# The first 28 pairs of a hybrid layer with activations stationary, and two jobs of POOL on VectorE

## The chip, the cores and the metric

The kernel runs on one core of one Trainium2 chip. The metric is the device time of one execution in microseconds (us); three runs of the kernel before gave 2392.42, 2395.93 and 2392.65, median 2392.65.

The core has five engines that run beside each other and wait for one another through semaphores: TensorE (PE; its weight loads are PEld), VectorE (DVE), ScalarE (ACT), GpSimd (POOL) and SyncE (SP), which here issues the DMAs.

## The reference

One layer on 256 positions of width 2048, in float32: a feed-forward, a mixer (differential attention beside a gated delta rule) and a second feed-forward. Each is preceded by a shift and scale and followed by a gate, a residual and a layer norm; shift, scale and gate come from c through `w_ada`.

```python
def swiglu_ffn(h, w_in, w_out):
    g, u = jnp.split(h @ w_in, 2, axis=-1)
    return (jax.nn.silu(g) * u) @ w_out

ada = (silu(c) @ w_ada[l] + b_ada[l]).reshape(B, 3, 3, D)
shift, scale, gate = ada[:, :, 0, None], ada[:, :, 1, None], ada[:, :, 2, None]
y = swiglu_ffn(x * (1 + scale[:, 0]) + shift[:, 0], w_ffn_in[l, 0], w_ffn_out[l, 0])   # 2048 -> 2*5632 -> 2048
x = layer_norm(ALPHA * x + 0.5 * gate[:, 0] * y, ln_g[l, 0], ln_b[l, 0])
y = hybrid_mixer(x * (1 + scale[:, 1]) + shift[:, 1], ...)
x = layer_norm(ALPHA * x + gate[:, 1] * y, ln_g[l, 1], ln_b[l, 1])
y = swiglu_ffn(x * (1 + scale[:, 2]) + shift[:, 2], w_ffn_in[l, 1], w_ffn_out[l, 1])
x = layer_norm(ALPHA * x + 0.5 * gate[:, 2] * y, ln_g[l, 2], ln_b[l, 2])
```

## The kernel before

**Split products.** A float32 matrix is split into a high part (`hi`, rounded by ACT) and a low part (`lo` = raw - hi, by VectorE or POOL). A product takes three matmuls, hi·hi, hi·lo and lo·hi (`mm3`, lines 147 to 149), summed in a PSUM bank of 512 columns.

**Weights.** All weights come in one planned order as chunks of 128 x 1024 (512 KB). SP loads a chunk into one of six `raw` buffers, ACT writes `hi`, VectorE or POOL `lo` (`_split`), into one of four buffers each; PE reads them and frees the buffer. `k.pool_lo` says which engine makes the low part: 0 VectorE, 1 POOL for every chunk, 2 POOL for every second. Instructions go through a helper, so nearly all of VectorE, ACT and POOL show as line 88.

**Two forms of product.** With weights stationary, a matmul loads 128 x 128 of a chunk and streams h, 256 columns; a chunk is 24 matmuls (`_products`). With activations stationary, it loads 128 x 128 of h and streams 512 columns of weights; a chunk is 12 matmuls (`_xprod`, `_xstat`). The results of the first lie hidden by token, as the next product wants them; those of the second lie token by hidden and are turned by PE transposes (`hT`).

**The first stage.** h, the input of the first feed-forward, isn't there at the start: its 16 tiles come one by one (`_first_h`): four ada chunks (`sar`) each, four VectorE dots, `hf` on VectorE, `h_hi` on ACT, `h_lo` on POOL. Meanwhile the first 28 of the 44 pairs (a pair is 128 columns of g and of u) are computed in six visits (`VISITS`): each takes the tiles of h that are there, and adds its bank to an accumulator in SBUF (`acc`). `START_LO` gives the visits' `pool_lo`. A pair's last visit ends in `_ffn_hid`: add (VectorE), silu (ACT), multiply (VectorE), hi (ACT), lo (VectorE). The other 16 pairs of this feed-forward, and all of the last one, are made four at a time with activations stationary (`_ffn_block`, with `hT`).

**Beside the products.** `_Ada` makes the later shifts, scales and gates: per chunk `ar` two `acc<-ar,cs` steps on VectorE; a finished quarter of a gate is split (`acchi`, `acclo`) and summed over partitions by two matmuls of PE, `aps`. `_load_x` fetches the residual x for the mixer's and the last feed-forward's end and applies the norm's g and b, row by row (`rowg`, `rowb`): on POOL, 16 instructions each time. `_Next` makes the next layer's h at a layer's end; its stage 0 sets `pool_lo` to 1, so POOL makes the low parts during the last output product, and its `rest` sets it back.

**What sets the order.** The program keeps a model time `k.t`, which advances with PE's products; the rest are threads that yield how long they need, and after each `mm3` the threads that are due issue their next instructions. The order on each engine is fixed by this when the program is built.

Of the kernel before, what the change touches and what calls it, by code (L numbers as in the profile page):

```python
# [744 lines left out]
def _ffn_hid(k, ps, hid, j, acc=None, back=1):  # L745

    hid.job(j, k.read(_ffn_hid_run(k, ps, hid, j, acc, hid.all[-1:]), back))


def _ffn_hid_run(k, ps, hid, j, acc, before):  # L750
    u = k.uid()
    g, up = ps[:, 0, :], ps[:, 1, :]
    if acc is not None:
# [1 line left out]
        k.V.tensor_tensor(acc, acc, ps, ALU.add)
        g, up = acc[:, 0, :], acc[:, 1, :]
    yield 0.2
    while not all(th.done for th in before):
        yield 0.3
    sg = k.hp.tile([128, S], F32, tag="sg", name=f"sg{u}", bufs=2)  # L760
    k.A.activation(sg, g, AF.Silu)
    yield
    hf = k.hp.tile([128, S], F32, tag="hidf", name=f"hidf{u}", bufs=2)
    k.V.tensor_tensor(hf, sg, up, ALU.mult)
    yield
    both = k.hp.tile([128, 2, S], F32R, tag=f"hid{j}", name=f"hid{u}")
    hid[0][j], hid[1][j] = both[:, 0, :], both[:, 1, :]
    k.A.activation(hid[0][j], hf, AF.Copy)
    yield
    k.V.tensor_tensor(hid[1][j], hf, hid[0][j].bitcast(F32), ALU.subtract)  # L770


def _ffn_block(k, h, hid, b, before, pre):
# [36 lines left out]
    if pre is None:  # L810
        _xstat(k, KT // 2, h, gate)
    else:
        for t in range(2):
            k.read(gate(t, pre[t], 0, 512), 2 - t)
    _xstat(k, KT // 2, h, up)
# [675 lines left out]
def tile_hybrid_block(ctx: ExitStack, tc: tile.TileContext, names, aps):  # L1491
# [83 lines left out]
    def start(h, hid, side):  # L1575

        with ExitStack() as st:
# [5 lines left out]
            accs = [k.hp.tile([128, 2, S], F32, tag=f"hid{j}", name=f"acc{j}") for j in range(hid.ready)]  # L1583
            k.pool_lo = 1
            for (kt0, n, ja, jb), lo in zip(VISITS, START_LO):
                h.need(k, kt0)
# [1 line left out]
                npair, nchunk = max(1, 4 // n), max(1, n // 4)
                last = kt0 + n == KT
                for j0 in range(ja, jb, npair):  # L1590
                    pss = [k.bank([128, 2, S], "mms") for q in range(npair)]
                    for c in range(nchunk):
                        w = [x.rearrange("p (q r) -> p q r", q=npair) for x in k.weights()]
                        for q, ps in enumerate(pss):
                            _products(k, ps, [x[:, q, :] for x in w], kt0 + 4 * c, n // nchunk, [h, h], c == 0,
                                      c == nchunk - 1)
                    for q, ps in enumerate(pss):
                        j = j0 + q
                        if last:
                            _ffn_hid(k, ps, hid, j, accs[j], npair - q)  # L1600
                        else:
                            k.read(add(accs[j], ps, kt0 == 0), npair - q)
                    if last and first is not None:
                        k.wait(lambda: first.done)
                        first = None
                        _ada_keep(k)
                        st.close()
                        ada = side()
# [64 lines left out]
def _layout(inputs, np):  # L1673
# [40 lines left out]
    for kt0, n, ja, jb in VISITS:
        m, q = min(n, 4), max(1, 4 // n)
        w = wi[0][kt0 * 128:(kt0 + n) * 128, ja * 256:jb * 256].reshape(n // m, m, 128, (jb - ja) // q, q, 256)
        first.append(w.transpose(3, 0, 2, 4, 1, 5).reshape(-1, 128, 1024))
# [47 lines left out]
```

## Time and profile before

| | |
|---|---|
| median of three runs | 2392.65 us |
| the profiled execution | 2389.68 us, span 2387.9 |
| PE busy | 2305.5 us, 97% |
| PEld busy | 2071.9 us, 87% |
| VectorE busy | 1707.0 us, 71% |
| ACT busy | 1033.1 us, 43% |
| POOL busy | 329.1 us, 14% |
| DMA | 581.7 MB, mean 244 GB/s |
| chain that ended last | PE 86%, VectorE 7%, issue 2% |
| first and last matmul of the first stage | 15.6 and 360.7 us |

Busy time is no proof of a bound: a busy PE can be slow or fast, and an engine at 70% can be late at one place. So the pace of a product is read from how far apart its chunks stand, a stall from a window in which PE is less than fully busy, and its cause from what PE waited for there. "Clock" is the share of TensorE's full clock that was granted.

### The profile page before, as it was taken

The numbers are of one execution on the slowest core, as the hardware profiler recorded it, in microseconds if no ns is written. First come the engines' busy times: TensorE is split into PE (matmuls) and PEld (weight loads), VectorE is DVE, ScalarE is ACT, GpSimd is POOL, SyncE is SP. The second block draws the span as 40 slices with busy tenths as digits, with TensorE's granted clock in tenths as the row PEclk, the third lists the DMA queues.
The fourth block names the chain that finished last, engine by engine and source line by source line (L and its number), as shares of the span: only waits on it lengthen the run. The fifth ranks groups of instructions, "written<-read, shape, count | busy, mean of one in ns | idle before, by whom it ended". The sixth has DMA issues, their size and how long they took to land.

```text
span 2387.9 us, 36796 instructions
## 1 busy us (share of the span) xinstructions
PE 2305.5 (97%) x14217; PEld 2071.9 (87%) x14217; DVE 1707.0 (71%) x2508; ACT 1033.1 (43%) x1390; POOL 329.1 (14%) x218
## 2 busy tenths in 40 slices
PE   6999999999999899999999999999999999999997
PEld 6999997888888889988999999987878888888886
DVE  5667888787775688878887887786787555544556
ACT  4434444434444444454444434444444443444432
POOL 5884000000001310000000220013050000000001
PEclk8999999999999999999999999999999999999999
DMA  9998878899875566454546888876888556655553
GB/s 362 332 327 292 300 250 274 305 339 322 315 267 189 176 204 209 157 173 149 170 162 244 298 296 306 286 282 204 310 302 309 189 192 194 193 187 192 188 187 111
DMA packets 166359, 581.70 MB, mean 244 GB/s; under 512 B 19820, under 2 KB 22812, under 8 KB 165416
## 3 DMA queue, kind: packets, MB, share of 16 engines
q1 hardware_dynamic: 166184, 579.36, 70.7%
q8 instruction: 111, 1.82, 0.3%
q14 instruction: 64, 0.52, 0.1%
HBM read 572.98 MB, written 7.88 MB: 243 GB/s over the span
## 4 chain that ended last, share of the span: by engine, by line
PE 86%; DVE 7%; issue 2%; DMA 1%; POOL 1%; ACT 1%; SPq 0%; DVEq 0%; ACTq 0%; POOLq 0%
PE mx L148 17%; PE mx L147 17%; PE mx L149 17%; PE mm L147 6%; PE mm L148 6%; PE mm L149 6%; PE mms L148 4%; PE mms L149 4%; PE mms L147 4%; DVE lo L88 2%; DVE acc L88 1%; PE UY L153 1%; DVE x L88 1%; ACT hi L88 1%; PE hT L158 1%
## 5 line engine op out<-in xcount | busy, mean ns | idle before, releaser
L88 ACT ACTIVATE hi<-raw 128x1024 fp32r<-128x1024 f32 x769 | 811.6, 1059 | 968.7 <-PE mx L149 669.3
L88 DVE TENSOR_TENSOR lo<-raw,hi 128x1024 fp32r<-128x1024 f32 x690 | 855.7, 1246 | 495.7 <-ACT hi L88 485.4
L147 PE MATMUL mx<-hi,h_hi 128*128 128x512 f32 x992 | 389.7, 393 | 0.0
L149 PE MATMUL mx<-hi,h_lo 128*128 128x512 f32 x992 | 387.2, 390 | 0.0
L148 PE MATMUL mx<-lo,h_hi 128*128 128x512 f32 x992 | 387.0, 390 | 0.0
L147 PE MATMUL mm<-h_hi,hi 128*128 128x256 f32 x1216 | 354.4, 291 | 0.0
L149 PE MATMUL mm<-h_hi,lo 128*128 128x256 f32 x1216 | 346.5, 285 | 3.4 <-DVE lo L88 3.4
L148 PE MATMUL mm<-h_lo,hi 128*128 128x256 f32 x1216 | 346.4, 285 | 0.0
L88 POOL TENSOR_TENSOR lo<-raw,hi 128x1024 fp32r<-128x1024 f32 x79 | 190.2, 2415 | 788.0 <-ACT hi L88 788.0
L147 PE MATMUL mx<-hi,hid 128*128 128x512 f32 (+1 forms) x768 | 285.1, 371 | 1.4 <-ACT hi L88 1.4
L148 PE MATMUL mx<-lo,hid 128*128 128x512 f32 (+1 forms) x768 | 284.7, 371 | 0.8 <-DVE lo L88 0.8
L149 PE MATMUL mx<-hi,hid 128*128 128x512 f32 (+1 forms) x768 | 284.5, 370 | 0.0
L147 PE MATMUL mms<-h_hi,hi 128*128 128x256 f32 x896 | 256.2, 286 | 10.2 <-ACT hi L88 5.9
L148 PE MATMUL mms<-h_lo,hi 128*128 128x256 f32 x896 | 256.2, 286 | 3.7 <-POOL h_lo L88 3.7
L149 PE MATMUL mms<-h_hi,lo 128*128 128x256 f32 x896 | 255.9, 286 | 1.6 <-POOL lo L88 1.6
L149 PEld LDWEIGHTS mm<-h_hi,lo 128*128 128x128 f32 x1216 | 235.2, 193 | 3.9 <-DVE lo L88 3.9
L147 PEld LDWEIGHTS mm<-h_hi,hi 128*128 128x128 f32 x1216 | 235.7, 194 | 1.7 <-issue 1.6
L148 PEld LDWEIGHTS mm<-h_lo,hi 128*128 128x128 f32 x1216 | 235.7, 194 | 0.7 <-issue 0.6
L149 PEld LDWEIGHTS mx<-hi,h_lo 128*128 128x128 f32 x992 | 186.6, 188 | 39.2
L147 PEld LDWEIGHTS mx<-hi,h_hi 128*128 128x128 f32 x992 | 186.7, 188 | 38.2 <-issue 0.2
L148 PEld LDWEIGHTS mx<-lo,h_hi 128*128 128x128 f32 x992 | 186.7, 188 | 38.0 <-issue 0.2
L147 PEld LDWEIGHTS mms<-h_hi,hi 128*128 128x128 f32 x896 | 174.4, 195 | 10.9 <-ACT hi L88 6.1
(304 smaller groups left out, 3236.2 us busy)
## 6 DMA issues: line engine op xcount, KB each, us to landing
raw<-in_w_ffn_in_dram SPq DMA_DIRECT2D x240, 512.0 KB, 4.7
raw<-in_w_ffn_out_dram SPq DMA_DIRECT2D x176, 512.0 KB, 4.1
raw<-in_w_first_dram SPq DMA_DIRECT2D x112, 512.0 KB, 5.0
ar<-in_w_gate_dram SPq DMA_DIRECT2D x96, 512.0 KB, 5.1
ar<-in_w_ada_dram SPq DMA_DIRECT2D x96, 512.0 KB, 5.1
sar<-in_w_ada_dram SPq DMA_DIRECT2D x64, 512.0 KB, 5.0
raw<-in_w_gab_dram SPq DMA_DIRECT2D x64, 512.0 KB, 4.5
raw<-in_w_kq_dram SPq DMA_DIRECT2D x32, 512.0 KB, 3.6
```

The source lines that it names most:

```text
L88: return f(*args, **kw)
L147: mm(ps, lhsT=lhs[0], rhs=rhs[0], start=start, stop=False, skip_group_check=True)
L148: mm(ps, lhsT=lhs[0], rhs=rhs[1], start=False, stop=False, skip_group_check=True)
L149: mm(ps, lhsT=lhs[1], rhs=rhs[0], start=False, stop=stop, skip_group_check=True)
L153: self.nc.tensor.matmul(ps, lhsT=lhsT, rhs=rhs, start=start, stop=stop, skip_group_check=True)
L158: self.nc.tensor.transpose(ps, src, self.ident if ident is None else ident)
```

## The change

**The first stage.** `VISITS` now counts blocks of four pairs (0 to 7) and the visits run with activations stationary: a new `_xbanks` makes two banks (one for each half of the tokens) from the chunks of a visit, for g and for u. The columns of all visits, the count of chunks and the adds into `acc` are as before; `w_first` is laid out to match. `_ffn_hid` goes: a block's last visit ends in `_ffn_block`, which adds to `acc` (`summed`), applies silu and multiply on 512 columns, and turns the result on PE (`hT`).

**The affine part.** In `_load_x` the sixteen products and sums with `rowg` and `rowb` go from POOL to VectorE, and each waits 2 us of model time for itself.

**A layer's end.** `pool_lo` is not set to 1 in `_Next.step`; the low parts there are VectorE's. The setting ahead of the first visit goes as well, so the first two low parts of the kernel are VectorE's.

```diff
-VISITS = ((0, 2, 0, 28), (2, 2, 0, 28), (4, 4, 0, 28), (8, 4, 0, 12), (8, 8, 12, 28), (12, 4, 0, 12))
+VISITS = ((0, 2, 0, 7), (2, 2, 0, 7), (4, 4, 0, 7), (8, 4, 0, 3), (8, 8, 3, 7), (12, 4, 0, 3))
...
+def _xbanks(k, kt0, n, act, name="mx"):
+
+    pss = [k.bank([128, 512], name) for _ in range(2)]
+    for c in range(n // 2):
+        w = k.weights()
+        for j in range(2):
+            for t in range(2):
+                _xprod(k, pss[t], w, act, kt0 + 2 * c + j, j, t, 0, 512, kt0 + n - 1, kt0)
+    return pss
...
         if stage == 0:
-            k.pool_lo = 1
             self.A = None
...
-        yield 8.0
+        yield 4.0
         for t in range(2):
-            k.P.tensor_tensor(x[t][:, sl], x[t][:, sl], g, ALU.mult)
-            k.P.tensor_tensor(x[t][:, sl], x[t][:, sl], b, ALU.add)
+            for v, op in ((g, ALU.mult), (b, ALU.add)):
+                yield 2.0
+                k.V.tensor_tensor(x[t][:, sl], x[t][:, sl], v, op)
...
-def _ffn_block(k, h, hid, b, before, pre):
+def _ffn_block(k, hid, b, before, banks, accs=None):
     sg = {}
-    def gate(t, ps, lo, hi):
+    def summed(i, t, ps):
+        if accs is None:
+            return ps
+        acc = accs[4 * b + 2 * i + t]
+        k.V.tensor_tensor(acc, acc, ps, ALU.add)
+        return acc
+
+    def gate(t, ps):
         yield 0.2
+        src = summed(0, t, ps)
         while not all(th.done for th in before):
             yield 0.3
         sg[t] = k.hp.tile([128, 512], F32, tag=f"sg{t}", name=f"sg{k.uid()}")
-        k.A.activation(sg[t], ps, AF.Silu)
+        k.A.activation(sg[t], src, AF.Silu)
-    def up(t, ps, lo, hi):
+    def up(t, ps):
         yield 0.2
-        k.V.tensor_tensor(sg[t], sg[t], ps, ALU.mult)
+        src = summed(1, t, ps)
+        while t not in sg:
+            yield 0.3
+        k.V.tensor_tensor(sg[t], sg[t], src, ALU.mult)
...
-            k.pool_lo = 1
-            for (kt0, n, ja, jb), lo in zip(VISITS, START_LO):
+            for (kt0, n, ba, bb), lo in zip(VISITS, START_LO):
                 h.need(k, kt0)
                 k.pool_lo = lo
...
+                for b in range(ba, bb):
+                    if kt0 + n < KT:
+                        for i in range(2):
+                            for t, ps in enumerate(_xbanks(k, kt0, n, h, "mms")):
+                                k.read(add(accs[4 * b + 2 * i + t], ps, kt0 == 0), 2 - t)
+                        continue
...
+                    _ffn_block(k, hid, b, hid.all[-1:], banks, accs)
```

What stands in PE's order near the end of the first stage, in the last visit, around the `aps` pair of a gate's quarter. `mms` is a bank of the stage. Before:

```order
L147 MATMUL mms_4066<-h_hi_91,hi_3950 128x256
L148 MATMUL mms_4066<-h_lo_92,hi_3950 128x256
L149 MATMUL mms_4066<-h_hi_91,lo_3951 128x256
L153 MATMUL aps_4108<-acchi_4095,ones 128x512
L153 MATMUL aps_4108<-acclo_4096,ones 128x512
L147 MATMUL mms_4115<-h_hi_91,hi_3988 128x256
L148 MATMUL mms_4115<-h_lo_92,hi_3988 128x256
L149 MATMUL mms_4115<-h_hi_91,lo_3989 128x256
```

After:

```order
L147 MATMUL mms_2816<-hi_2741,h_hi_91 128x512
L148 MATMUL mms_2816<-lo_2742,h_hi_91 128x512
L149 MATMUL mms_2816<-hi_2741,h_lo_92 128x512
L153 MATMUL aps_2859<-acchi_2834,ones 128x512
L153 MATMUL aps_2859<-acclo_2835,ones 128x512
L158 MATMUL hT_2863<-ident,sg_2811 128x128
L158 MATMUL hT_2863<-ident,sg_2813 128x128
L158 MATMUL hT_2863<-ident,sg_2811 128x128
L158 MATMUL hT_2863<-ident,sg_2813 128x128
L147 MATMUL mms_2868<-hi_2770,h_hi_91 128x512
```

The `aps` pair now follows the two g banks of the last visit's second block; behind it come the first transposes of the block ahead of it, whose `sg` VectorE writes.

The affine part in the mixer's last part. Before it is in POOL's order (`x_13896` and `x_13897` are the two halves of the residual):

```order
L88 TENSOR_TENSOR x_13896<-x_13896,rowg_14315 128x512
L88 TENSOR_TENSOR x_13896<-x_13896,rowb_14316 128x512
L88 TENSOR_TENSOR x_13897<-x_13897,rowg_14315 128x512
L88 TENSOR_TENSOR x_13897<-x_13897,rowb_14316 128x512
L88 TENSOR_TENSOR x_13896<-x_13896,rowg_14430 128x512
```

After, in VectorE's order, between low parts and the ada gate's steps:

```order
L88 TENSOR_TENSOR lo_13052<-raw_12842,hi_13051 128x1024
L88 SCALAR_TENSOR_TENSOR acc_12854<-ar_12882,cs,acc_12854 128x512 x2
L88 TENSOR_TENSOR x_12552<-x_12552,rowg_12971 128x512
L88 TENSOR_TENSOR lo_13087<-raw_12888,hi_13086 128x1024
L88 TENSOR_TENSOR x_12552<-x_12552,rowb_12972 128x512
L88 TENSOR_TENSOR x_12553<-x_12553,rowg_12971 128x512
L88 TENSOR_TENSOR lo_13122<-raw_12921,hi_13121 128x1024
L88 TENSOR_TENSOR x_12553<-x_12553,rowb_12972 128x512
L88 SCALAR_TENSOR_TENSOR acc_12854<-ar_13007,cs,acc_12854 128x512 x2
L88 TENSOR_TENSOR lo_13161<-raw_12951,hi_13160 128x1024
```

Eight of the sixteen stand ahead of the next `acclo` there, eight behind it.

The end of the first layer in VectorE's order: the last low parts, and the residual of the output product's first tail piece. Before:

```order
L88 SCALAR_TENSOR_TENSOR res_7560<-mx_7376,gate_2789 128x512
L88 TENSOR_TENSOR x_2816<-x_2816,res_7560 128x512
L88 BN_STATS st_93<-x_2816 128x6 x2
L88 SCALAR_TENSOR_TENSOR res_7751<-mx_7539,gate_2789 128x256
L88 TENSOR_TENSOR x_2815<-x_2815,res_7751 128x256
```

After:

```order
L88 TENSOR_TENSOR lo_6330<-raw_6155,hi_6329 128x1024
L88 TENSOR_TENSOR lo_6360<-raw_6173,hi_6359 128x1024
L88 TENSOR_TENSOR lo_6390<-raw_6203,hi_6389 128x1024
L88 SCALAR_TENSOR_TENSOR res_6407<-mx_6195,gate_1986 128x256
L88 TENSOR_TENSOR x_2013<-x_2013,res_6407 128x256
```

The low parts of the last output product, which POOL made, stand ahead of the tail's first `res`.

## Rows read from the trace of the kernel before

**Rows 1.** Timeline of POOL, first stage (start, us, engine, line, operation, shape, idle before).
```profile
140.85 7.15 POOL L88 TENSOR_TENSOR lo<-raw,hi 128x1024 fp32r<-128x1024 f32 x3 [0.21 <-ACT hi L88]
...
154.30 0.74 POOL L88 TENSOR_TENSOR h_lo<-hf,h_hi 128x256 fp32r<-128x256 f32 x1 [0.68 <-DMA raw<-in_w_first_dram]
155.25 7.15 POOL L88 TENSOR_TENSOR lo<-raw,hi 128x1024 fp32r<-128x1024 f32 x3 [0.21 <-ACT hi L88]
```

**Rows 2.** Timeline of ACT, first layer, output product with 512 columns.
```profile
755.65 1.06 ACT L88 ACTIVATE hi<-raw 128x1024 fp32r<-128x1024 f32 x1 [1.66 <-PE mx L149]
758.37 1.06 ACT L88 ACTIVATE hi<-raw 128x1024 fp32r<-128x1024 f32 x1 [1.66 <-PE mx L149]
```

**Rows 3.** Windows: stretch, length, PE, PEld, DVE, ACT, POOL busy, clock, DMA share, GB/s.
```profile
100.00:150.00 50.00, 50.00 (x418) 49.97 (x418) 34.40 (x52) 18.98 (x20) 43.88 (x21) 1.00 0.92 335
...
300.00:350.00 50.00, 45.59 (x356) 44.79 (x355) 42.97 (x63) 21.80 (x34) 0.00 (x0) 0.93 0.75 251
350.00:400.00 50.00, 45.99 (x242) 38.58 (x241) 42.06 (x59) 23.11 (x34) 0.00 (x0) 1.00 0.81 267
...
1350.00:1400.00 50.00, 46.69 (x361) 45.89 (x361) 46.73 (x40) 18.96 (x22) 26.80 (x15) 0.93 0.79 267
1400.00:1450.00 50.00, 48.74 (x402) 48.18 (x401) 42.02 (x51) 20.38 (x25) 0.00 (x0) 1.00 0.90 317
```

**Rows 4.** Windows of 5 us, columns as above.
```profile
45.00:50.00 5.00, 5.00 (x44) 5.00 (x43) 2.35 (x5) 3.31 (x5) 4.39 (x2) 1.00 1.03 409
...
335.00:340.00 5.00, 2.70 (x9) 2.10 (x10) 3.97 (x7) 2.13 (x5) 0.00 (x0) 0.63 0.75 229
...
1755.00:1760.00 5.00, 3.32 (x14) 2.20 (x12) 4.96 (x5) 2.11 (x3) 3.63 (x3) 1.00 0.98 349
1760.00:1765.00 5.00, 4.48 (x20) 3.71 (x21) 4.96 (x4) 1.66 (x2) 3.77 (x2) 1.00 0.88 350
```

**Rows 5.** Waits of PE, 290 to 400: total us, times, longest.
```profile
PE aps L153 <- ACT acchi L88: 4.4, 2, 3.5
PE aps L153 <- DVE acclo L88: 1.9, 2, 1.0
```

**Rows 6.** Timeline of VectorE (DVE), end of the first stage.
```profile
310.24 1.22 DVE L88 TENSOR_TENSOR lo<-raw,hi 128x1024 fp32r<-128x1024 f32 x1
...
313.49 1.23 DVE L88 TENSOR_TENSOR lo<-raw,hi 128x1024 fp32r<-128x1024 f32 x1 [1.10 <-ACT hi L88]
...
316.41 1.22 DVE L88 TENSOR_TENSOR lo<-raw,hi 128x1024 fp32r<-128x1024 f32 x1
...
337.35 0.69 DVE L88 TENSOR_TENSOR acclo<-acc,acchi 128x512 fp32r<-128x512 f32 x1
```

**Rows 7.** Chain of waits, last feed-forward: start, us, what.
```profile
1732.39 0.44 PE hT L158 x4
```

**Rows 8.** Timeline of POOL, affine part in the mixer: first and last of sixteen.
```profile
1347.01 2.27 POOL L88 TENSOR_TENSOR x<-x,rowg 128x512 f32<-128x512 f32 x1 [65.41 <-DMA rowg<-in_ln_g_dram]
...
1387.97 1.63 POOL L88 TENSOR_TENSOR x<-x,rowb 128x512 f32<-128x512 f32 x1
```

**Rows 9.** Timeline of VectorE beside them (thirteen longer rows, 1348.52 to 1388.47).
```profile
1348.52 1.85 DVE L88 TENSOR_TENSOR lo<-raw,hi 128x1024 fp32r<-128x1024 f32 x1 [0.39 <-ACT hi L88]
...
1357.06 1.53 DVE L88 SCALAR_TENSOR_TENSOR acc<-ar,cs,acc 128x512 f32<-128x512 f32 x2
...
1362.59 2.32 DVE L88 TENSOR_TENSOR lo<-raw,hi 128x1024 fp32r<-128x1024 f32 x1 [0.52 <-DMA raw<-in_w_gab_dram]
1364.83 3.48 DVE L88 SCALAR_TENSOR_TENSOR acc<-ar,cs,acc 128x512 f32<-128x512 f32 x2
...
1388.47 3.25 DVE L88 SCALAR_TENSOR_TENSOR acc<-ar,cs,acc 128x512 f32<-128x512 f32 x3
```

**Rows 10.** Timeline of VectorE, end of the first layer.
```profile
745.00 0.69 DVE L88 TENSOR_TENSOR x<-x,res 128x512 f32<-128x512 f32 x1
...
782.98 1.97 DVE L88 TENSOR_TENSOR x<-x,res 128x256 f32<-128x256 f32 x1
...
785.76 0.42 DVE L88 TENSOR_TENSOR x<-x,res 128x256 f32<-128x256 f32 x1
```

More of the change, by code (lines that the diff above doesn't have):

```diff
@@ L284, in _tile, with _xprod @@
     return part[kt] if isinstance(part, dict) else part[:, kt, :]
-def _xprod(k, ps, w, act, kt, j, t, lo, hi, last):
+def _xprod(k, ps, w, act, kt, j, t, lo, hi, last, first=0):
     act.need(k, kt)
@@ L292, in _xprod @@
     k.mm3(ps[:, lo:hi], (_tile(act[0], kt)[:, tk], _tile(act[1], kt)[:, tk]), (w[0][:, sl], w[1][:, sl]),
-          start=(kt == 0), stop=(kt == last))
+          start=(kt == first), stop=(kt == last))
     k.pump()
+def _xbanks(k, kt0, n, act, name="mx"):
[6 more added lines that the diff above has]
+    return pss
 def _xstat(k, n, act, done, tail=0):
@@ L740, in _y_blocks @@
         return finish.step(3, ada, ln)
[L745 to L753, printed above, removed]
-        yield 0.2
[L755 to L770, printed above, removed]
-def _ffn_block(k, h, hid, b, before, pre):
-    sg = {}
-    def gate(t, ps, lo, hi):
-        yield 0.2
+def _ffn_block(k, hid, b, before, banks, accs=None):
+    sg = {}
+    def summed(i, t, ps):
[5 more added lines that the diff above has]
+    def gate(t, ps):
+        yield 0.2
+        src = summed(0, t, ps)
         while not all(th.done for th in before):
@@ L808, in turn @@
                 k.V.tensor_tensor(hid[1][j], ps[:, q, :], hid[0][j].bitcast(F32), ALU.subtract)
[L810 to L815, printed above, removed]
+    for i, done in enumerate((gate, up)):
+        for t, ps in enumerate(banks(i)):
+            k.read(done(t, ps), 2 - t)
     th = k.spawn(turn(list(k.users[-2:])))
@@ L848, in _ffn, with banks @@
                     ada = side()
-            turned = []
+            turned = hid.all[-1:]
             for b in range(b0, size // 4):
-                turned = [_ffn_block(k, h, hid, b, turned, None if b or half else pre)]
+                def banks(i, b=b):
+                    return pre if pre and b == half == i == 0 else _xbanks(k, 0, KT, h)
+                turned = [_ffn_block(k, hid, b, turned, banks)]
             res = _y_blocks(k, size // 2, hid, ada, sub, half == 0, ln if half else None, finish, tail)
@@ L1575, in start @@
     def start(h, hid, side):
+        ada = None
         with ExitStack() as st:
@@ L1582, in start @@
             first.step()
-            accs = [k.hp.tile([128, 2, S], F32, tag=f"hid{j}", name=f"acc{j}") for j in range(hid.ready)]
-            k.pool_lo = 1
-            for (kt0, n, ja, jb), lo in zip(VISITS, START_LO):
+            accs = [k.hp.tile([128, 2, S], F32, tag=f"hid{j}", name=f"acc{j}").rearrange("p a b -> p (a b)")
+                    for j in range(hid.ready)]
+            for (kt0, n, ba, bb), lo in zip(VISITS, START_LO):
                 h.need(k, kt0)
                 k.pool_lo = lo
[L1588 to L1608, printed above, removed]
@@ new lines, in start, with banks @@
+                for b in range(ba, bb):
[4 more added lines that the diff above has]
+                        continue
+                    def banks(i):
+                        nonlocal first, ada
+                        pss = _xbanks(k, kt0, n, h, "mms")
+                        if first is not None:
+                            k.wait(lambda: first.done)
+                            first = None
+                            _ada_keep(k)
+                            st.close()
+                            ada = side()
+                        return pss
+                    _ffn_block(k, hid, b, hid.all[-1:], banks, accs)
@@ L1711, in _layout @@
         r[f"w_ffn_in{sub}"] = np.stack([chunks_x(wi[sub][:, DFF * i - j0:DFF * i]) for i in (1, 2)])
-    wi = [pair(w[:, :DFF], w[:, DFF:]) for w in wi]
     first = []
[L1714 to L1717, printed above, removed]
+    for kt0, n, ba, bb in VISITS:
+        w = wi[0][kt0 * 128:(kt0 + n) * 128]
+        w = np.stack([chunks_x(w[:, DFF * i + ba * 512:DFF * i + bb * 512]) for i in range(2)], 1)
+        first.append(w.reshape(-1, 128, 1024))
     r["w_first"] = np.concatenate(first, 0)
```

1 line of the change is left out of this document (removed).

## The prediction

> **What bounds the kernel now.** I read the page first (TensorE is busy 97% of the span, and 86% of the chain that ended last is PE), so a term counts only if it changes TensorE's pace or one of its waits. Then the places that the diff touches, in order of time.
>
> The pace, from two timelines. In the first stage POOL makes each low part and waits each time for PE to free a buffer, so its rows beat in PE's time: the same three-row group comes at 140.85 and at 155.25 with five chunks between, so a 512 KB chunk of weights costs PE 14.40/5 = 2.88 us, 0.120 for each of its 24 matmuls of 256 columns [rows 1]. Where activations are already stationary, ACT's high parts, each released by PE, stand 2.72 us apart: 0.227 for each of 12 matmuls of 512 columns [rows 2]. Both stretches have the clock at 2.4 GHz.
>
> The stalls, from windows. Full stretches of the first stage hold 418 matmuls in 50 us; 300 to 350 holds 356, with the clock at 0.93, and 350 to 400 has PE busy 45.99 of 50. In the mixer's last part 1350 to 1400 holds 361, again at 0.93, and VectorE is busy 46.73; 1400 to 1450 lacks another 1.3 us [rows 3]. In windows of 5 us the clock is at 0.63 from 335 to 340, so part of it ran at 1.2 GHz after PE had waited; the last feed-forward lacks 1.68 and 0.52 us near 1760 [rows 4]. In the first stall PE waited for the ada gate's sum, the aps pair (6.3 us, to ACT's acchi and VectorE's acclo) [rows 5]: VectorE was late. Its rows there recur every 6.17 us (310.24 to 316.41), while PE needs 5.76 for two chunks; 1.10 of the 6.17 is a wait for ACT's hi, which stands behind ACT's silu, and that behind VectorE's add. acclo comes at 337.35 [rows 6].
>
> **The change, part by part.** Sums are made against the profiled execution, 2389.68 us (span 2387.9 and 1.8 around it); the median shown, 2392.65, lies 2.97 above.
>
> *Pace of the first stage.* It has 112 chunks (28 pairs, 16 tiles, four of these products in a chunk). The columns stay; the matmuls and weight loads halve, 24 to 12, all in the form of rows 2. 2.88 - 2.72 = 0.16 us a chunk. The first two chunks run at 1.2 GHz, where the columns bound; 110 x 0.16 = 17.6. I take 17, since some tiles of h now come one chunk later in ACT's and POOL's order. The cover: POOL's cycle of five chunks and one tile of h ends when the next group starts; its work is three low parts in 7.15 (2.38 each), so five are 11.9, with 0.74 for h_lo 12.7, with the gaps some 13.0 of 14.40 [rows 1]. The new cycle is 13.6: POOL just keeps up. DMA moves 335 GB/s there [rows 3] and would need 335 x 2.88/2.72 = 355; it has moved 409 [rows 4]. If POOL or DMA do bind, only the last 50 chunks, where POOL has little left, gain: 50 x 0.16 = 8, the low end.
>
> By the Trainium skill (TensorE: Matmul & The Clock Gate, Back-to-back issue gap) a warm matmul takes its columns over 2.4 GHz plus 2.5 ns, which gives 109 and 216 ns, by estimate 0.03 us a chunk and 3.5 us here: the page speaks against most of this term. The trace does not agree: 120 and 227 ns, 13 ns above the bare columns each time, so halving the count is worth 13 ns and not 2.5.
>
> *Transposes.* Each of 7 blocks of four pairs adds 8 transposes on PE. Four take 0.44 us in the last feed-forward [rows 7]: 14 x 0.44 = 6.2 us, all on the path. Each also makes PE wait for VectorE's sg, where before nothing of a pair came back to PE until the output product; queued behind it are the next matmuls, and behind these ACT's next hi. Bounds: nothing further, to a stall like that of rows 5 for each block (the slow rival).
>
> *VectorE at the end of the first stage.* Two multiplies of 512 replace four of 256, two silus replace four, so one ACT round trip serves two pairs. From rows 6: 6.17 less half of 1.10 is 5.6 for two chunks, against PE's 5.44 + 0.22 of transposes. VectorE then stops falling behind in the long visit; in the last one, with an add for every chunk, it still does. At the aps pair (after the first bank of the second-last block) VectorE has to get two adds, two ada steps, two hid rows, a lo, two sg and acclo done in PE's two chunks, 5.44 us; it is late there by some microseconds again. Before, the stage end lost 62 matmuls x 0.12 = 7.4 us and 4.0 us [rows 3]; I take two thirds of 11.4 for after, a gain of 4, with bounds -2 and +9.
>
> *The affine part on VectorE.* POOL's sixteen products and sums run from 1347.01 to 1390 [rows 8]. Thirteen VectorE rows between 1348.52 and 1388.47 are longer than their like: a lo 2.32 (1.22 in rows 6), lo 1.85, two ada steps 3.48 (1.53); the excess of the thirteen sums to 14.6 us [rows 9]. VectorE has a row of this form alone at 0.69 (x<-x,res, 745.00) [rows 10]: 16 x 0.69 = 11.0 us, spread over some 50 us. So VectorE gets 3.6 us back, and by the aps pair in this stretch, before which 11.3 of the 14.6 fall now and half of the sixteen then, 11.3 - 5.5 = 5.8 us, more than PE's wait of 3.3 there; the clock then has no cause to fall. Lost before: 57 matmuls x 0.12 = 6.8, then 1.3 [rows 3]. I take 6 of these 8.1. In the last feed-forward the same happens with 2.2 lost [rows 4]; I take 1.5. Together 7.5, bounds 0 (VectorE as late as now) and 10.3. The row loads are issued 6 us of the planner's time ahead of their use, so VectorE should not wait on them.
>
> By the Trainium skill (SBUF — State Buffer, Who interferes with whom) a VectorE instruction with two SBUF inputs and a GpSimd instruction that reads SBUF lock each other out for a whole instruction. The 1.1 us on a lo fits that.
>
> *Low parts at a layer's end.* VectorE sits idle ahead of the tail there, so seven lo of 1.22 are hidden. POOL's last one overlaps the first x of the tail, which takes 1.97 instead of 0.42 [rows 10]; this x is on the chain to the norm. Now a lo of 1.22 stands ahead of it, at about the time of the old one's start: some 0.7 us earlier, at two layer ends 1.4, bounds 0 and 3. At the start VectorE also makes the first two low parts, ahead of the next ada dots; DMA is the limit there [rows 4], so I take 0, bounds -2 and +2.
>
> *Sum.* 17 - 6.2 + 4 + 7.5 + 1.4 = 23.7. 2389.68 - 23.7 = 2366.0 for the profiled execution, 2369 for the median.
>
> **Rivals.**
> 1. *The first stage is bound by POOL or DMA.* For: POOL would be busy 13.0 of 13.6, DMA 0.92 busy [rows 3]. Against: POOL still waits for ACT, that is PE, in each cycle. The pace gives 8: 2378.
> 2. *The affine part only moves the stall.* VectorE is at 84% after it, 42.0 of 50 [rows 3], and the x rows stand ahead of acclo. Against: the 14.6 taken away. Gain 0 there: 2376.5.
> 3. *The transposes stall PE: slower.* Place: the 7 blocks; mechanism: add, silu and multiply not done when PE comes to the first hT, 3.5 chunks after a block. At the price of the known stall, 7 x 7.4 = 52: 2421. It decides from 23.7/7 = 3.4 us a block. For: VectorE is the late engine there. Against: 3.5 chunks are 9.5 us, and the two hT groups of a block wait little in later stages.
> 4. *The change doesn't do what it says to the pace:* the 13 ns belong to this stage and not to the count of matmuls. For it only the formula's 3.5 us; against it rows 2, the same form. 2382.5.
> 5. *Rivals 1 and 2 together, with the stage end worse by 2:* 8 - 6.2 - 2 + 0 + 1.4 = 1.2, so 2391: no change.
>
> **Chances.** Forecast 0.60; rivals 1: 0.14, 2: 0.12, 3: 0.05, 4: 0.03, 5: 0.06. What can be told from no change is 0.2%, 4.8 us. Faster by more: forecast, 1, 2 and 4, 0.89; within: 0.06; slower: 0.05. The forecast's own range is 2361 to 2377 (stage end -2 to +9, affine 0 to 10). The range for 8 in 10 takes in 1, 2 and 4: 2358 to 2384.
>
> **What would show it.** Chunks 2.72 us apart from 35 us on; the first stage's last matmul near 345 instead of 360.7; POOL's low parts nearly back to back for the first 56 chunks. hT groups in it with 0.44 and little wait in front; a shorter or missing window below full clock near 335 and near 1380; VectorE's lo at 1.22 throughout the mixer's last part; the first x of a tail at 0.42. Wrong would be: chunks at 2.88 with POOL or DMA full, PE idle ahead of hT for over 3 us at most blocks, or acclo as late as now.

## The result, and the profile after

The changed kernel takes 2356.59 us (median of four runs, 2354.36 to 2357.71) beside 2392.94 for the kernel before on the same chip: a ratio of 0.984, 95% interval 0.983 to 0.986. That is 36.4 us faster, where 23.7 were forecast and the range ended at 2358. The direction and the places are as forecast; the time lies 1.4 us outside the range, mainly because two terms were too small. Span against span it is 2387.9 and 2352.5, 35.4 us.

The same windows as in [rows 3], of the kernel after:

```profile
100.00:150.00 50.00, 50.00 (x222) 41.19 (x221) 36.86 (x54) 21.25 (x23) 46.68 (x23) 1.00 0.99 362
...
300.00:350.00 50.00, 47.99 (x223) 39.40 (x223) 47.51 (x67) 26.56 (x39) 0.00 (x0) 1.00 0.79 260
350.00:400.00 50.00, 48.53 (x213) 38.32 (x212) 40.97 (x53) 21.15 (x25) 0.00 (x0) 1.00 0.86 279
...
1350.00:1400.00 50.00, 50.00 (x416) 49.82 (x415) 44.68 (x58) 21.48 (x26) 0.00 (x0) 1.00 0.82 296
1400.00:1450.00 50.00, 50.00 (x417) 49.91 (x416) 43.07 (x54) 21.47 (x26) 0.00 (x0) 1.00 0.88 323
```

The clock stays at 1.00 in every row, PE is never idle in the mixer's last part, and at the first stage's end it is idle for 2.0 and 1.5 us, where the kernel before lost 7.4 (counted in matmuls) and 4.0. POOL is fuller (46.68) and DMA moves 362 GB/s, and neither holds PE up. POOL's timeline, which answers to [rows 1] (start, us, operation, wait):

```profile
123.05 4.79 POOL L88 TENSOR_TENSOR lo<-raw,hi 128x1024 fp32r<-128x1024 f32 x2
...
135.95 0.74 POOL L88 TENSOR_TENSOR h_lo<-hf,h_hi 128x256 fp32r<-128x256 f32 x1
136.64 4.79 POOL L88 TENSOR_TENSOR lo<-raw,hi 128x1024 fp32r<-128x1024 f32 x2
141.75 2.42 POOL L88 TENSOR_TENSOR lo<-raw,hi 128x1024 fp32r<-128x1024 f32 x1 [0.31 <-ACT hi L88]
144.48 2.40 POOL L88 TENSOR_TENSOR lo<-raw,hi 128x1024 fp32r<-128x1024 f32 x1 [0.31 <-ACT hi L88]
```

Five chunks take 136.64 - 123.05 = 13.59, 2.72 each, and POOL still waits 0.3 us for most low parts: it keeps up with little to spare. A group of transposes in PE's timeline:

```profile
245.43 0.60 PE L158 MATMUL hT<-ident,sg 128*128 128x128 f32 x4
245.78 0.48 PE L147 MATMUL mms<-hi,h_hi 128*128 128x512 f32 x1
246.10 0.40 PE L148 MATMUL mms<-lo,h_hi 128*128 128x512 f32 x1
```

From the group's start to the second matmul behind it are 0.67 us, 0.23 of them the first matmul's: 0.44, as in [rows 7]. PE's waits between 240 and 360 us (total, times, longest), beside [rows 5]:

```profile
PE aps L153 <- DVE acclo L88: 2.0, 1, 2.0
PE hT L158 <- DVE sg L88: 0.8, 2, 0.5
```

VectorE's timeline at that aps pair shows why 2.0 us are left: it goes from one instruction to the next without a gap, and acclo comes behind both sg.

```profile
321.19 1.21 DVE L88 TENSOR_TENSOR lo<-raw,hi 128x1024 fp32r<-128x1024 f32 x1
322.32 1.28 DVE L88 TENSOR_TENSOR sg<-sg,acc 128x512 f32<-128x512 f32 x2
323.52 0.68 DVE L88 TENSOR_TENSOR acclo<-acc,acchi 128x512 fp32r<-128x512 f32 x1
```

In the mixer's last part, which answers to [rows 9], VectorE's lo and the affine rows are short, side by side:

```profile
1328.14 0.68 DVE L88 TENSOR_TENSOR x<-x,rowg 128x512 f32<-128x512 f32 x1
1328.74 1.22 DVE L88 TENSOR_TENSOR lo<-raw,hi 128x1024 fp32r<-128x1024 f32 x1
1329.88 0.68 DVE L88 TENSOR_TENSOR x<-x,rowb 128x512 f32<-128x512 f32 x1
```

At the first layer's end, the first x of the tail takes 0.43 and not 1.97 [rows 10], right behind VectorE's last lo:

```profile
762.30 1.22 DVE L88 TENSOR_TENSOR lo<-raw,hi 128x1024 fp32r<-128x1024 f32 x1 [1.66 <-ACT hi L88]
763.44 0.42 DVE L88 SCALAR_TENSOR_TENSOR res<-mx,gate 128x256 f32<-128x256 f32 x1
763.89 0.43 DVE L88 TENSOR_TENSOR x<-x,res 128x256 f32<-128x256 f32 x1
```

To place the gain in time I compare when the same instructions come in each kernel's profiled execution. This table, made from the timelines, serves all experiments. "Stage ends" is the start of the first stage's last matmul, "first lnt" that of the first transpose at the first layer's end (tile lnt). "GB" is the mixer's middle, from the first GB matmul to the last; "gth" its last part, from the first instruction on gth to the last; "rest" runs from the last lnt matmul (second layer end) to the end, with the last feed-forward in it. The ratio to the kernel before, measured on the same chip, stands beside them.

| kernel | stage ends | first lnt | GB | gth | rest | ratio, interval |
|---|---|---|---|---|---|---|
| before | 360.7 | 789.5 | 300.5 | 256.0 | 745.7 | 1 |
| after | 342.6 | 768.9 | 297.3 | 247.1 | 742.6 | 0.984 (0.983-0.986) |
| affine_pool | 342.3 | 768.6 | 300.6 | 255.4 | 749.6 | 0.992 (0.990-0.993) |
| affine_only | 360.7 | 789.5 | 297.3 | 247.0 | 742.9 | 0.994 (0.993-0.996) |
| ends_pool | 342.6 | 769.6 | 300.6 | 247.1 | 742.6 | 0.986 (0.984-0.987) |
| stage_only | 342.5 | 769.6 | 300.4 | 254.7 | 747.5 | 0.991 (0.990-0.993) |
| halves | 358.5 | 783.8 | 304.7 | 247.1 | 742.9 | 0.991 (0.990-0.993) |
| turns_twice | 346.5 | 771.1 | 307.4 | 247.6 | 742.7 | 0.986 (0.985-0.988) |
| before_lo2 | 363.2 | 791.3 | 304.7 | 255.8 | 749.0 | 1.000 (0.999-1.001) |
| after_lo2 | 343.4 | 770.4 | 301.9 | 247.7 | 742.6 | 0.985 (0.983-0.986) |
| no_add | 359.9 | 785.5 | 304.8 | 255.3 | 749.6 | 0.998 (0.997-0.999) |
| pool_dummy | 343.4 | 768.5 | 300.4 | 252.3 | 743.8 | 0.987 (0.986-0.989) |
| pool_memset | 342.6 | 768.8 | 297.2 | 247.4 | 742.6 | 0.985 (0.983-0.986) |
| gate7 | 339.7 | 764.2 | 300.4 | 247.4 | 742.6 | 0.984 (0.982-0.985) |
| half_ada | 353.2 | 777.9 | 302.9 | 253.8 | 750.2 | 0.996 (0.994-0.997) |
| half_ada_after | 340.7 | 765.1 | 301.5 | 247.1 | 742.6 | 0.983 (0.982-0.985) |
| gate7_before | 359.2 | 782.7 | 304.8 | 254.7 | 749.7 | 0.997 (0.996-0.998) |
| gate8 | 340.4 | 765.3 | 297.3 | 247.1 | 742.6 | 0.983 (0.982-0.985) |

From before to after the first lnt matmul comes 20.6 us earlier, gth is 8.9 shorter and the rest 3.1; 3.2 come from GB, where PE's order is the same in all the kernels, and -0.4 lies in between.

### The profile page after: what moved, and what is told of

Same layout as the page of the kernel before. It is cut to its first block, busy times and chain, and to the rows that moved or that the text cites. A ratio compares the mean times of both kernels' runs of the same rounds, so it can differ in the third digit from the quotient of the medians.

```text
span 2352.5 us, 34147 instructions
## 1 busy us (share of the span) xinstructions
PE 2284.1 (97%) x12929; PEld 1997.7 (85%) x12929; DVE 1708.1 (73%) x2542; ACT 1031.0 (44%) x1376; POOL 230.6 (10%) x170
## 4 chain that ended last, share of the span: by engine, by line
PE 90%; DVE 5%; issue 1%; ACT 1%; DMA 1%; POOL 1%; SPq 0%; DVEq 0%; ACTq 0%; POOLq 0%
PE mx L147 17%; PE mx L149 17%; PE mx L148 17%; PE mm L147 7%; PE mm L148 7%; PE mm L149 7%; PE mms L149 4%; PE mms L147 4%; PE mms L148 4%; DVE lo L88 1%; PE hT L158 1%; PE UY L153 1%; DVE x L88 1%; ACT hi L88 1%; PE pre L147 1%
## 5 line engine op out<-in xcount | busy, mean ns | idle before, releaser
L147 PE MATMUL mms<-hi,h_hi 128*128 128x512 f32 x448 | 177.5, 396 | 11.4 <-ACT h_hi L88 5.8
L149 PE MATMUL mms<-hi,h_lo 128*128 128x512 f32 x448 | 176.5, 394 | 1.2 <-POOL h_lo L88 1.2
L148 PE MATMUL mms<-lo,h_hi 128*128 128x512 f32 x448 | 176.3, 394 | 0.5 <-DVE lo L88 0.5
L149 PEld LDWEIGHTS mx<-hi,hid 128*128 128x128 f32 x768 | 144.7, 188 | 26.4 <-DVE hid L88 1.6
L147 PEld LDWEIGHTS mx<-hi,hid 128*128 128x128 f32 x768 | 144.8, 189 | 25.1 <-issue 0.6
```

What stands on the lines that cost most here:

```text
L147: mm(ps, lhsT=lhs[0], rhs=rhs[0], start=start, stop=False, skip_group_check=True)
L148: mm(ps, lhsT=lhs[0], rhs=rhs[1], start=False, stop=False, skip_group_check=True)
L149: mm(ps, lhsT=lhs[1], rhs=rhs[0], start=False, stop=stop, skip_group_check=True)
```

## The experiments

### The parts, one at a time

Two kernels undo one part of the change, two make one part alone.

```diff
 # affine_pool (after), and the other way round affine_only (before)
-        yield 4.0
+        yield 8.0
...
-                k.V.tensor_tensor(x[t][:, sl], x[t][:, sl], v, op)
+            k.P.tensor_tensor(x[t][:, sl], x[t][:, sl], g, ALU.mult)
+            k.P.tensor_tensor(x[t][:, sl], x[t][:, sl], b, ALU.add)
 # ends_pool (after): pool_lo back to 1 in step, to 0 in rest
+            k.pool_lo = 1
 # stage_only: both edits, and pool_lo = 1 ahead of the first visit
```

> The changed kernel with the affine part back on POOL (sixteen products and sums each time, 8 us after the row loads). Theory: the part is worth what the anchors of the two traces show, 8.4 us between the first and the last gth matmul (236.9 before, 228.5 after) and about 2.5 us in the last feed-forward: 2356.6 + 10.9 = 2367.5, with gth's stretch back at 237 and a window near 1360 with the clock under full. Rival (the size on record): 7.5, so 2364. Rival (the stretch got shorter because it is reached earlier or because of the other parts): 2357 to 2359, gth's stretch still 229 to 231.

> The kernel before with only the affine part moved to VectorE. Theory: -10.9, 2392.9 - 10.9 = 2382.0; gth's stretch 228.5 in place of 236.9; the first stage as before (last matmul 360.7). Rival (size on record): -7.5, 2385.4. Rival (the gain needs the new first stage): 2391 to 2393.

> The changed kernel with the low parts at a layer's end back on POOL. Theory: about 0.9 to 1.4 us slower, 2357.5 to 2358.0, and the first x of each tail back at 1.97 us. Rival (the tail's chain doesn't gain from it): 2356.6, nothing to be told apart. Rival (the 3.3 us that the stretch between the first and last GB matmul lost come from it, 300.5 to 297.3): 2360 or more, that stretch back at 300.5.

> The kernel before with only the new first stage (affine part and low parts at a layer's end on POOL). Theory: the first lnt matmul 20.7 us earlier than before (789.5), of which pace 17.5, transposes -6.2, start 0.8, stalls at the stage's end 8.5 (11.4 before, 3.5 left less rounding): 2392.9 - 20.6 = 2372.3. Rival (sizes on record, 17 - 6.2 + 4): 2378. Rival (the parts add up to less than the whole, as one stall covers for another): gth's stretch shorter than 236 without its own edit, 2365.

Measured: 2374.89, 2379.96, 2359.57 and 2374.28, beside 2394.92 for the kernel before. The parts are independent: but for GB, each stretch of the table falls into one of two narrow groups, by whether its own edit is there. The whole times add up too: 20.6 us (stage_only), 15.0 (affine_only) and 1.0 (ends_pool against the changed kernel) make 36.6 of the 36.4. All ten kernels with the affine part on VectorE and POOL's reads out of the way have gth at 247.0 to 247.7 and the rest at 742.6 to 742.9; all with it on POOL have 253.8 to 256.0 and 745.7 to 750.2. The layer ends are worth 0.7 us each (first lnt 769.6 and 768.9; from the last gth to the last lnt 104.8 and 104.1), the size on record, and the tail's first x is back at 1.97 in ends_pool. The rival that GB's 3.2 us come from them falls: affine_only has 297.3 too.

affine_pool lost some 16 us by medians, not 10.9 (it is 20.0 faster than the kernel before on its chip, the changed kernel 36.4). The kernel before was profiled in an execution with a good last feed-forward. In five other kernels with the affine part on POOL the rest took 747.5 to 750.2. In all five the clock falls behind the wait at this aps pair (0.50 to 0.78 in a row of 5 us), and in four the wait itself is longer, 3.8 to 4.0 us in place of 2.1. Windows of affine_pool:

```profile
1735.00:1740.00 5.00, 1.79 (x7) 0.93 (x5) 4.96 (x4) 1.58 (x2) 4.92 (x3) 0.95 0.98 372
1740.00:1745.00 5.00, 4.30 (x10) 3.43 (x11) 3.20 (x4) 0.60 (x1) 0.85 (x2) 0.50 0.88 252
1745.00:1750.00 5.00, 5.00 (x20) 4.01 (x20) 2.41 (x2) 2.12 (x2) 4.09 (x4) 0.87 0.52 184
```

PE is idle for 3.2 and 0.7 us here (2.7 before acclo and 1.2 before acchi), and then runs at 1.2 GHz (0.50 in the second row); in [rows 4] 1.7 and 0.5 passed without a fall. So the part is worth 8.9 + 3.1 = 12.0 against the execution shown, and 15 to 16 by medians (affine_only: 2394.92 to 2379.96).

### Is the pace one of the count?

```diff
+                for lo in (0, 256) if name == "mms" else (0,):
+                    _xprod(k, pss[t], w, act, kt0 + 2 * c + j, j, t, lo, lo + 256 if name == "mms" else 512, ...)
-                _xprod(k, pss[t], w, act, kt0 + 2 * c + j, j, t, 0, 512, ...)
```

> The changed kernel with each matmul of the first stage cut into two of 256 columns (activations still stationary, 24 matmuls and weight loads in a chunk; everything else as in the changed kernel). Theory: the pace goes with the count of matmuls, 13 ns each: chunks at 2.88 us again, 110 x 0.16 = 17.6 us slower, the stage's last matmul near 360, 2374. Rival (the 0.16 us belong to the old form, weights stationary, not to the count): chunks at 2.72, 2357. Rival (a fixed cost of 2.5 ns for each matmul): 3.5 us, 2360.

The two halves of a bank share it here, and part of the first stage's sums is not kept; matmuls, loads and order are as said. Measured: 2373.07 (before 2393.28). Its low parts on POOL:

```profile
133.64 2.41 POOL L88 TENSOR_TENSOR lo<-raw,hi 128x1024 fp32r<-128x1024 f32 x1 [0.48 <-ACT hi L88]
136.52 2.41 POOL L88 TENSOR_TENSOR lo<-raw,hi 128x1024 fp32r<-128x1024 f32 x1 [0.47 <-ACT hi L88]
```

2.88 us a chunk again, with activations stationary: the 13 ns belong to each matmul with its weight load (the two were cut together, and no run separates them). The stage ends 15.9 us later, and PE waits 1.4 us less for VectorE in it (aps 1.2 and hT 0.2, where it was 2.0 and 0.8), so the pace itself is some 17.3. Rival 4 is out. The Trainium skill (TensorE: Matmul & The Clock Gate, Back-to-back issue gap) has 2.5 ns as the fixed part of an isolated warm matmul, and says that this formula is not the spacing in a stream of weight loads and matmuls, for which it gives 131 ns at 512 columns. This kernel is such a stream, so the formula wasn't the one to take; neither figure fits it, with 13 ns and 227 ns measured.

### The transposes

```diff
-                    k.tr(ps[:, q, ...], sg[t][:, ...])
+                    for _ in range(2 if accs else 1):
+                        k.tr(ps[:, q, ...], sg[t][:, ...])
```

> The changed kernel with every transpose of the first stage's blocks made twice (14 more groups of four). Theory: a group costs its 0.44 us of PE and no stall, 14 x 0.44 = 6.2: the stage's last matmul at 348.3 to 348.8, 2362.8. Rival (the transposes hide beside waits of PE): under 2 us. Rival (each is a place where PE waits for VectorE and the clock can fall): 10 us and more.

Measured: 2362.02, the stage's end 3.9 us later. PE's waits for VectorE shrink at the same time from 2.8 to 0.9 us (one line, aps), and 3.9 + 1.9 = 5.8: the groups cost what was expected, but where VectorE is late, PE's own work fills a wait. By the first lnt matmul 2.2 us are left of 6.2. That the whole time came near the 2362.8 expected is luck: of the 10.6 us between the two profiled executions 10.1 lie in GB (307.4 and 297.3).

### Why PE waited at the stage's end

First, relief for VectorE through POOL, in both kernels.

```diff
-START_LO = (1, 1, 1, 2, 0, 0)
+START_LO = (1, 1, 1, 2, 0, 2)
```

> The kernel before with POOL making every second low part in the last visit of the first stage (24 chunks, about 277 to 360 us), 12 x 1.22 = 14.6 us off VectorE. Theory: the wait at the aps pair (6.3 us), the clock's fall behind it and the 4.0 us after 360 come from VectorE being late there: most of the 11.4 us goes, 2382 to 2385, last matmul of the stage near 353. Rival (POOL's 2.4 us low parts hold up VectorE's instructions for as long as they save, as in rows 9): 2392 to 2394. Rival (the wait is ACT's or comes from where the pair stands in PE's order): aps still waits over 4 us.

> The changed kernel with POOL making every second low part in the last visit of the first stage. Theory: the 3.5 us still lost there (2.0 at the aps pair, 1.5 between 350 and 365) go, 2353 to 2355, below both kernels. Rival (POOL's low parts hold up VectorE as much as they save): 2357 or more, with new waits of PE before hT or aps.

Measured: 2392.20 (before 2393.28) and 2356.62: nothing gained. The last visit has 12 chunks, not 24, so POOL made six low parts in each run and not twelve, in before_lo2 only two of them ahead of the aps pair. These two start at 326.50 (5.76 us), and VectorE's timeline beside them reads:

```profile
326.44 3.56 DVE L88 SCALAR_TENSOR_TENSOR acc<-ar,cs,acc 128x512 f32<-128x512 f32 x2
329.92 3.42 DVE L88 TENSOR_TENSOR lo<-raw,hi 128x1024 fp32r<-128x1024 f32 x1
...
341.75 2.40 DVE L88 TENSOR_TENSOR hidf<-sg,acc 128x256 f32<-128x256 f32 x1 [0.26 <-ACT sg L88]
```

Alone these take 1.53, 1.22 and 0.42, so they are 6.2 us longer. The help is paid back at once, so the run doesn't tell whether VectorE's lateness was the cause. Second, VectorE's adds of the last visit left out:

```diff
-        k.V.tensor_tensor(acc, acc, ps, ALU.add)
-        g, up = acc[:, 0, :], acc[:, 1, :]
+        if j >= 12:
+            k.V.tensor_tensor(acc, acc, ps, ALU.add)
+            g, up = acc[:, 0, :], acc[:, 1, :]
```

> The kernel before; it leaves out the add of acc for the twelve pairs of the last visit (VectorE, 12 x 0.68 = 8.2 us; these pairs keep only the last visit's sum). It relieves VectorE at the stage's end without POOL. Theory: the wait of PE at the aps pair (6.3 us) and the fall of the clock come from VectorE being late: the wait falls under 2 us, the clock stays at 1.00 in 300 to 350, the stage ends 6 to 7.4 us earlier, near 354, about 2384 to 2387 in all. Rival (the wait is set by where the pair stands and by ACT's acchi): the wait stays over 4 us, 2392.

Measured: 2390.28 (before 2394.09). The wait at aps is gone, and another one has come, in PE's waits:

```profile
PE mms L147 <- DVE hidf L88: 3.9, 3, 1.9
PE mx L147 <- DVE hidf L88: 1.6, 2, 1.3
```

Without the add, the bank is freed only by the multiply, behind ACT's silu. This run is no proof either: the new waits themselves gave VectorE time. Its 3.8 us lie between what the theory and the rival gave. Third, work taken off VectorE without moving an instruction elsewhere, the second of each two steps of the first gate:

```diff
-                else:
+                elif (sub, kind) != (0, 2) or j == 0:
                     k.V.scalar_tensor_tensor(acc, w, c, acc, ALU.mult, ALU.add)
+                else:
+                    k.V.t = max(k.V.t, k.chain, k.t) + 0.08 + 1.04e-3 * 512
+                    k.chain = k.V.t + 0.13
```

> The kernel before; it leaves out every second acc<-ar,cs step of the first gate (0.75 us each, 31 in all from about 255 to 650 us, so half of that gate's sum is missing). No instruction moves on any engine. Theory (PE waits at the stage's end because VectorE is late): VectorE gets 0.75 us back in every 6 us, so it is never behind at the aps pair: wait under 1 us, clock 1.00 from 300 to 350, and most of the 7.4 + 4.0 us gone: first lnt matmul near 779 (789.5 before), the stage's end near 354, about 2382. Rival (the place of the pair in PE's order or ACT sets it): the wait stays over 4 us, 2391 or more.

> The changed kernel with the same steps left out (half of the first gate's sum is missing). Theory: only the 3.5 us that the changed kernel still loses are there to be had: first lnt matmul near 765.5 (768.9), stage's end near 340.6, 2353; with the run on the kernel before, this says that the change's gain at the stage's end (8 of 11.4 us) was VectorE's lateness. Rival: no change, 2356 to 2357.

Measured: 2383.75 (before 2394.22) and 2354.20. The window of half_ada, then PE's waits in it from 290 to 400:

```profile
300.00:350.00 50.00, 49.09 (x408) 48.74 (x407) 41.12 (x61) 24.85 (x40) 0.00 (x0) 1.00 0.81 280
```

```profile
PE aps L153 <- DVE acclo L88: 1.6, 2, 0.9
```

6.3 us of waiting become 1.6, the clock doesn't fall, and the first lnt matmul comes 11.6 us earlier (777.9). The order on PE, ACT, POOL and SP is the same, and VectorE's differs by the 32 steps alone, so this shows it: VectorE's lateness cost the kernel before at least 11.6 us in the profiles, 10.5 by medians. In the changed kernel the same relief is worth 3.8 (768.9 to 765.1). The difference, 7.8, is what the change gains at the stage's end; 4 was the term.

### Reading or working beside VectorE?

```diff
+            scr = ...                                 # a spare tile, 128 x 512
...
                 k.V.tensor_tensor(x[t][:, sl], x[t][:, sl], v, op)
+                k.P.tensor_tensor(scr, scr, scr, op)      # pool_dummy
+                for _ in range(4):                        # pool_memset, in its place
+                    k.P.memset(scr, 0.0)
```

> The changed kernel, and after each of the sixteen VectorE instructions of the affine part POOL does one product or sum of the same form on a spare tile (read from SBUF and written back, results unused; it touches no data of the kernel). The order on all other engines is as in the changed kernel. Theory (what the old form cost was that VectorE and POOL hold each other up when both read SBUF): VectorE's rows beside POOL's are longer again (lo 1.8 to 3.4 in place of 1.22), now with the affine part on top, so PE loses at least the 8.8 + 3.1 us of before: 2368 or more. Rival (the old form cost because the sum came late or through its place in the order): 2357, rows at 1.22.

> As the run with POOL's spare products and sums, but with four memsets of the spare tile in place of each (0.53 us each by the memset of bin, 34 us in all against 30): POOL is as busy and writes SBUF, but reads none. Theory: it is the reading that holds VectorE up: lo at 1.22, 2356 to 2358. Rival (any work of POOL at the side of VectorE costs): as with the products, 2368 or more.

Measured: 2363.81 and 2357.05. The spare work waits for nothing, so POOL did it in one piece, before the affine part came (16 products from 1260.30, 25.83 us; 64 memsets from 1258.46, 37.34 us). VectorE's groups between 1260 and 1287 (count, busy us, mean ns) of pool_dummy, then of pool_memset:

```profile
L88 DVE TENSOR_TENSOR lo<-raw,hi 128x1024 fp32r<-128x1024 f32 x9 | 15.8, 1768 | 3.3 <-ACT hi L88 3.3
L88 DVE SCALAR_TENSOR_TENSOR acc<-ar,cs,acc 128x512 f32<-128x512 f32 x5 | 7.3, 1457 | 0.1
```

```profile
L88 DVE TENSOR_TENSOR lo<-raw,hi 128x1024 fp32r<-128x1024 f32 x9 | 11.0, 1221 | 5.0 <-ACT hi L88 5.0
L88 DVE SCALAR_TENSOR_TENSOR acc<-ar,cs,acc 128x512 f32<-128x512 f32 x9 | 6.7, 749 | 0.8 <-DMA ar<-in_w_gate_dram 0.6
```

The order of the engines is the same, and so is the time in which POOL is busy in these 27 us (24.9 and 24.4). Beside POOL's products a lo takes 1.77 and a step 1.46; beside its memsets 1.22 and 0.75, as alone. gth is 5 us longer with the products and unchanged with the memsets. My 2368 was too much, as I read it because POOL didn't work where VectorE was fullest. By the Trainium skill (SBUF — State Buffer, Who interferes with whom) a VectorE instruction with two SBUF inputs contends with a GpSimd instruction that reads SBUF and not with one that only writes it; both runs agree.

### The first gate's steps, further apart

```diff
-GATE_PACE = 6.0
+GATE_PACE = 7.0        # gate7, gate7_before; 8.0 in gate8
```

> The changed kernel with the first gate's ada steps every 7 us of the planner's time in place of 6. VectorE is without a gap from 305 to 365 there; two steps of 1.53 us less fall into these 60 us. Theory: part of the 3.5 us that are still lost goes, 2354 to 2356, if the gate's last quarter is in time for the residual. Rival: the aps pairs come at places where PE waits as long or longer, 2357 to 2360.

> The kernel before with the first gate's steps every 7 us. Theory: VectorE is less late there too and the aps pair stands 97 matmuls later; 4 to 10 of the 11.4 us go, 2383 to 2389. Rival (VectorE is as late at the later pair): 2391 to 2394.

> The changed kernel with the first gate's steps every 8 us of the planner's time (6 in the changed kernel; at 7 the first lnt matmul came at 764.2 in place of 768.9). Theory: VectorE is no longer late at the stage's end, nothing left to gain beyond 7: first lnt matmul at 763.5 to 764.5, 2352 to 2356. Rival (the gate's last quarter comes too late for the residual of the first feed-forward): first lnt matmul later than 768.9, 2358 or more.

Measured: 2355.73, 2385.76 and 2353.33. In gate8 PE waits for nothing between 200 and 400 us:

```profile
300.00:350.00 50.00, 50.00 (x236) 41.35 (x235) 48.02 (x67) 26.31 (x40) 0.00 (x0) 1.00 0.76 242
350.00:400.00 50.00, 50.00 (x222) 40.58 (x221) 36.07 (x44) 21.52 (x24) 0.00 (x0) 1.00 0.81 257
```

The first lnt matmul comes 4.7 (gate7) and 3.6 us (gate8, 765.3, 0.8 behind what was expected) earlier than in the changed kernel, and a later gate delays nothing. In whole times the gain doesn't show apart from the spread (0.983 and 0.984, intervals that overlap). In the kernel before the slower steps bring 8.5 us, the first lnt matmul at 782.7.

## Why the prediction was wrong in size

| term | forecast | measured |
|---|---|---|
| pace of the first stage | 17 | 17.3 to 17.6 |
| transposes | -6.2 | -6.2 of work |
| stalls at the stage's end | 4 | 7.8 |
| affine part | 7.5 | 12.0 (15 to 16 by medians) |
| two layer ends | 1.4 | 1.4 |
| start | 0 | about 0.8 |
| mixer's middle | none | 3.2, by the clock |

**What held.** Chunks at 2.72; the cover by POOL and DMA, so rival 1 is out; transposes at 0.44 without a stall like that of [rows 5], so rival 3 is out; the layer ends. At 50 us 95 of 1344 matmuls are done, where 176 of 2688 were: 0.6 chunks more, 1.6 us, half of it the pace and the other half the start's 0.8.

**The step that failed: the discounts on VectorE's lateness.** "it is late there by some microseconds again ... I take two thirds of 11.4 for after, a gain of 4" and "I take 6 of these 8.1". The first was worth 7.8, the second 8.9, and the affine part in all 12.0 to 16 where 7.5 stood. In the second place the working itself said that VectorE gets 5.8 us back by the aps pair, more than the 3.3 that PE waits; then the wait goes altogether, with the clock's fall behind it, and a discount has no ground. It went altogether: gth shows no wait of PE, and rival 2 is out. At the stage's end the lateness did stay, as 2.0 us, but the clock's fall behind a wait of 6 us, and most of what followed, went: between 300 and 343 us VectorE waits 2.7 us for ACT's hi, where it waited 6.2, as the prediction's one ACT round trip for two pairs would have it. That the clock holds behind the 2.0 us is not certain: pool_dummy has the same stage and the same wait, and there it fell (0.69 from 325 to 330), at no cost by the first lnt matmul (768.5).

**The bound that failed: 10.3 for the affine part.** The last feed-forward's 2.2 us were read as PE's idle time. Counted in matmuls it is more, as the same place shows in the kernel before and in the changed one:

```profile
1730.00:1860.00 130.00, 127.80 (x573) 105.04 (x572) 104.64 (x107) 57.96 (x70) 29.96 (x16) 1.00 0.85 299
```

```profile
1697.70:1827.70 130.00, 130.00 (x586) 107.51 (x585) 102.93 (x124) 59.17 (x71) 0.00 (x0) 1.00 0.86 304
```

13 x 0.227 = 3.0, which is the 3.1 of the table. The clock is 1.00 in both; a matmul's row is 0.39 to 0.50 us long where the next one comes after 0.227, so the end of one before a wait and the start of one behind it count as busy. In [rows 3] the same goes for 1400 to 1450, 402 of 417, 1.8 and not 1.3. Even so the bound would have been 11.6, below the 15 to 16 by medians: in six of the seven profiles with the part on POOL the last feed-forward loses more than in the one that the prediction read, as the clock falls there.

**The range.** The forecast's own ended at 2361, with both terms at their upper ends. (Its other end, 2377, was not made so: both terms at their lower ends give 2382.5.) Both hang on VectorE's lateness, and both came out near or beyond their upper ends. By medians the remaining 4 us are the affine part beyond its bound (15.0 against 10.3) and the start, less the 1.2 that the stage's end stayed under its own. That the median lies just outside 2358 and not inside is chance, as GB alone varies by more; that the two terms were too small is not.

**The mixer's middle.** Between the GB matmuls 3.2 us came that no edit explains. affine_only has the same instructions up to there as the kernel before, at the same times. Windows of the kernel before, and then of affine_only:

```profile
1061.80:1066.80 5.00, 3.35 (x30) 3.15 (x28) 1.01 (x3) 3.33 (x17) 0.00 (x0) 1.00 0.29 105
1066.80:1071.80 5.00, 3.25 (x22) 2.92 (x23) 4.62 (x17) 2.61 (x7) 0.00 (x0) 0.83 0.01 3
1071.80:1076.80 5.00, 5.00 (x37) 5.00 (x37) 3.75 (x12) 1.18 (x2) 0.00 (x0) 0.82 0.68 210
```

```profile
1061.80:1066.80 5.00, 3.32 (x29) 3.12 (x28) 1.00 (x3) 3.37 (x17) 0.00 (x0) 1.00 0.39 105
1066.80:1071.80 5.00, 3.29 (x28) 2.96 (x29) 4.64 (x16) 2.67 (x8) 0.00 (x0) 1.00 0.01 3
1071.80:1076.80 5.00, 5.00 (x44) 5.00 (x44) 3.72 (x13) 2.51 (x3) 0.98 (x3) 1.00 0.73 224
```

PE waits alike in both, and in one the clock falls and in the other it doesn't. What decides it was not found. So these 3.2 us are luck in the pair of profiles that is compared. By the medians, in which such chances are spread, the parts measured alone add up to the gain without them (36.6 and 36.4).

## What to carry to other kernels

Where one late engine causes several stalls, work out at each place whether the relief exceeds its lateness; if it does (5.8 us against 3.3 here), the stall and the clock's fall behind it go whole, and the terms err together, so add their bounds rather than discount each. Read what a stall costs by counting matmuls against a full stretch (3.0 us here), as idle time alone (2.2) leaves out matmuls that end or start beside it. Moving an elementwise job from GpSimd to VectorE can make VectorE faster, where GpSimd's reads stretch VectorE's instructions by more than the job costs (14.6 us against 11.0 here).

## What was not expected of the hardware

The same stretch of code (GB, PE's order the same in all) took from 297.2 to 307.4 us in 18 profiled executions, with a granted clock of 0.99 in the shortest and 0.96 in the longest: single profiles can differ by 10 us where nothing was changed. Memsets that kept GpSimd busy for 37 us beside VectorE cost VectorE nothing, while products that read SBUF stretched a lo from 1.22 to 1.77 us on average.
